# Experts of block 1: a ring of eleven weight slots until the fourth pair, and gathers and projections queued behind a pair's last input matmul

## The chip, the cores and the metric

The kernel runs on one core of a Trainium2 chip. The metric is the device time of one execution in microseconds (us). TensorE (PE) does the matmuls, VectorE (DVE), ScalarE (ACT) and GpSimd (POOL) the elementwise work, and SyncE (SP) issues the transfers of weights from HBM to SBUF, in one queue that is worked off in its order.

## The reference

Two blocks follow one another. Each mixes 256 tokens of width 1024 and then runs a layer of experts. The change touches the experts of block 1, 32 of them in four groups, with two chosen for each token in one group:

```python
for e in range(N_EXPERTS):
    a = jax.nn.silu(tok @ w_gate[e]) * (tok @ w_up[e])     # 1024 -> 512, twice
    out = out + combine[:, e:e + 1] * (a @ w_down[e])      # 512 -> 1024
```

`combine` holds the router's two weights of a token and zeros. Block 2's mixer needs projections of a second input, the context, which do not depend on block 1:

```python
h_ctx @ w_in        # one part of it, "xbc", is computed beside the experts of block 1
```

## The kernel before

**Pairs of experts.** `block1_moe` works through 16 pairs of experts. Each expert takes at most 32 tokens at first (a loop over a list, at L1685, does the others; it runs no iteration here). For a pair, PE multiplies the gathered tokens by eight *input pieces* of weights of 1 MB each (in0 to in3, for expert a and expert b; L1584). The *gated chain* follows: DVE L1471, three ACT operations, DVE L1473 and L1474, the transpose L1483 on PE, and the copy to `aT` on ACT. Then come four *output pieces* (out0, out1, each a and b; L1607), the multiplication into `y` on DVE, and the sum over tokens, `combine` (L1499 on PE, L1505 on DVE). `pd` and L1597 prepare the matrix for it.

**The weights' slots.** `Weights` holds the 1 MB pieces. `fetch` issues the next piece of a fixed list into the next slot of a fixed list: first the `first` slots, then the `ring` again and again. `n`, `w`, `za`, `zb`, `l`, `m`, `h0` and so on are names of regions in SBUF, and a piece's DMA waits on SP until the work that read that region before is done. Since SP has one queue, all that stands behind waits too. At pair 3 (`OVER`) the kernel fetches ahead what the loop over the list may disturb, runs the loop, and goes on with a ring of eight slots: `l` and `m` leave it, and `h1`, `g`, `g` join it.

**The gathers.** `Gather` picks the tokens of a range of experts with a one-hot matmul (L1352, `select` and `gather`, k = 0 to 7 for eight slices of the width). Experts 0 to 7 are gathered inside pair 0, 8 to 23 after pair 1's combine, and 24 to 31 after pair 2's.

**The context's projections.** `early()` takes the next step of `block2_ctx`. From pair 3 (`EARLY`) on it is called twice a pair: after the gated chain is written, and after the combine. A step issues two 0.5 MB loads `w_xbc` on SP (L365), splits them on ACT (L374) and DVE (L375), and multiplies them on PE: 32 matmuls of L403 and 16 of L407 a pair.

**Order on the engines.** A scheduler orders the instructions of each engine by its own estimates. `behind(pr, i)` tells it to put what is issued inside it after instruction `i`, where both are on one engine; it adds no wait of its own.

Of the kernel before, what the change touches and what calls it, by code (L numbers as in the profile page):

```python
# [28 lines left out]
EARLY = 3  # L29
# [504 lines left out]
def spread(pr, name, t):  # L534

    ap = pr.gains[name]
    pr.nc.sync.dma_start(t, bass.AP(tensor=ap.tensor, offset=ap.offset, ap=[[0, 128], [1, 1024]]))
    return t
# [819 lines left out]
class Gather:  # L1358
# [23 lines left out]
        gathered(self.pr, self.xhl, self.P, 32 * lo, 32 * hi - 32 * lo, self.gain, self.shift, k,  # L1382
                 self.tiles[key][:, o:o + 32 * hi - 32 * lo])

    def run(self, lo, hi):
        self.select(lo, hi)
        for k in range(8):
            self.gather(lo, hi, k)

    def __call__(self, k, e):  # L1390
# [45 lines left out]
def block1_weights(pr):  # L1436
    def piece(pi, s, j):
        for e in (2 * pi, 2 * pi + 1):
            yield (pi, s, j), pr.ins["wi" if s == "in" else "wd"][e, j]

    def order():


        for pi in range(16):
            js = [("in", k2) for k2 in range(4)] + [("out", h) for h in range(2)]
            for s, j in js if pi else js[:1] + js[4:] + js[1:4]:
                yield from piece(pi, s, j)
    ring = ["n"] * 2 + ["w"] * 3 + ["l", "m"]
    return order(), ["n"] * 2 + ["za"] * 3 + ["zb"] * 2 + ring[2:] + ["h0", "h1", ("hx", "hx"), ("zd", "y")], ring


def block2_weights(pr):
# [36 lines left out]
def behind(pr, i):  # L1489

    return pr.tc.issue_after(i.ins) if i is not None else nullcontext()
# [18 lines left out]
def block1_moe(pr, early):  # L1510
    nc, ins = pr.nc, pr.ins
    x = pr.x
    m1 = pr.mod1.rearrange("p (s k r) -> p s k r", s=6, r=2)
    gain, shift = (lambda k: pr.A2[:, k:k + 1]), (lambda k: m1[:, 3, k, 0:1])
    L = pr.L
    xhl = normed_split(pr, x, pr.r2)
    gl, el = L[:, :, 0:4], L[:, :, 4:36]
    b2 = lambda t, n: t[:, :, None].to_broadcast([128, 2, n])
    t2 = lambda n: pr.small(2, n)
    r3 = lambda t, n: t[:, 0:2 * n].rearrange("p (t e) -> p t e", t=2)  # L1520

    gm, gs, gw = t2("gm"), t2("gs"), t2("gw")
    nc.vector.tensor_reduce(gm, gl, AX.X, OP.max)
    ge = r3(pr.small(8, "ge8"), 4)
    nc.vector.tensor_sub(ge, gl, b2(gm, 4))
    nc.scalar.activation(ge, ge, AF.Exp)
    nc.vector.tensor_reduce(gs, ge, AX.X, OP.add)
    nc.vector.reciprocal(gw, gs)
    og = r3(pr.small(8, "og8"), 4)
    onehot_first(pr, og, gl, gm)  # L1530
    nc.vector.tensor_scalar(og, og, -1.0, -NEG, op0=OP.add, op1=OP.mult)

    em = pr.small(64, "em")
    e4 = em.rearrange("p (t g e) -> p t g e", t=2, g=4)
    nc.vector.tensor_add(e4, el.rearrange("p t (g e) -> p t g e", g=4),
                         og[:, :, :, None].to_broadcast([128, 2, 4, 8]))
    em = r3(em, 32)
    O, W, E = (pr.keep([128, 2, 32], n) for n in ("O", "W", "E"))
    m8 = pr.small(16, "m8").rearrange("p (t j) -> p t j", t=2)
    for t in range(2):  # L1540
        nc.vector.max(m8[:, t], em[:, t])
    two = pr.small(16, "two").rearrange("p (t j) -> p t j", t=2)
    nc.gpsimd.memset(two, -2.0 * NEG)
    nc.vector.tensor_copy(two[:, :, 0:2], m8[:, :, 0:2])
    for t in range(2):
        nc.vector.match_replace(E[:, t], two[:, t], em[:, t], 3.0 * NEG)
    nc.vector.tensor_tensor(O, E, em, op=OP.not_equal)
    pos = pr.keep([128, 2, 32], "pos")
    positions(pr, pos, O, 32)

    wb = t2("wb")
    nc.vector.tensor_sub(wb, m8[:, :, 1], m8[:, :, 0])
    nc.scalar.activation(wb, wb, AF.Exp)
    nc.vector.tensor_scalar(wb, wb, 1.0, None, op0=OP.add)
    nc.vector.reciprocal(wb, wb)
    nc.vector.tensor_mul(wb, wb, gw)
    nc.vector.tensor_sub(W, em, b2(m8[:, :, 0], 32))
    nc.scalar.activation(W, W, AF.Exp)
    nc.vector.tensor_mul(W, W, b2(wb, 32))
    nc.vector.tensor_mul(W, W, O)  # L1560
    pr.dbg("combine", W)
    xe = Gather(pr, pos, xhl, 32, gain, shift, [(("xa", "zc"), 0, 8), (("za", "za"), 8, 24), (("za",), 24, 32)])
    g2 = spread(pr, "g2", pr.new("g2", "g2"))
    moe = pr.moe[0]
    for pi in range(16):
        if pi == OVER:
            moe.fetch(7)
            overflow(pr, li, pos, W, xhl, gain, shift, x, g2)

            for tag in ("l", "m"):  # L1570
                moe.ring.remove(tag)
            moe.ring.extendleft(["h1", "g", "g"])
        es = (2 * pi, 2 * pi + 1)
        p = pr.ps("d")
        if pi == 0:
            xe.select(0, 8)
        for k2 in range(4):
            w = moe.take(pi, "in", k2)
            for k in (2 * k2, 2 * k2 + 1):
                if pi == 0:  # L1580
                    xe.gather(0, 8, k)
                for g in range(4):
                    e = es[g % 2]
                    nc.tensor.matmul(p[32 * g:32 * g + 32], xe(k, e), w[g % 2][2 * (g // 2) + k % 2],  # L1584
                                     start=k == 0, stop=k == 7, tile_position=(0, 32 * g))
        a = gated(pr, p, 64)
        if pi >= EARLY:
            early()
        aT = down_inputs(pr, a, 64)
        p = pr.ps("t")  # L1590
        for t in range(2):
            v = xe.P[t][:, 64 * pi:64 * pi + 64].rearrange("p (e j) -> p e j", e=2)
            d = pr.small(128, "pd")
            nc.gpsimd.tensor_mul(d.rearrange("p (e r j) -> p e r j", e=2, r=2),
                                 v[:, :, None, :].to_broadcast([128, 2, 2, 32]),
                                 W[:, t, 2 * pi:2 * pi + 2, None, None].to_broadcast([128, 2, 2, 32]))
            nc.tensor.transpose(p[:, 128 * t:128 * t + 128], d, pr.ident)  # L1597
        PWT = pr.small(256, "PWT")
        nc.scalar.activation(PWT, p[:, 0:256], AF.Copy)
        y = pr.new("y", "y")  # L1600
        for h in range(2):
            p = pr.ps("m")
            w = moe.take(pi, "out", h)
            for i in range(2):
                for g in range(4):
                    z = 64 * (2 * (g % 2) + i) + 32 * (g // 2)
                    nc.tensor.matmul(p[32 * g:32 * g + 32], aT[:, z:z + 32], w[g // 2][2 * (g % 2) + i],  # L1607
                                     start=i == 0, stop=i == 1, tile_position=(0, 32 * g))
            nc.vector.tensor_mul(y[:, 512 * h:512 * h + 512], p, g2[:, 512 * h:512 * h + 512])
        for h in range(2):  # L1610
            combine(pr, x, PWT, y, h, False, then=last if pi == 15 else None)
        if pi in (1, 2):
            xe.run(*((8, 24), (24, 32))[pi - 1])
        if pi == 0:
            li = overflow_list(pr, O)
        if pi >= EARLY:
            early()
        if pi == 4:
            fg = bcast(pr, "fin", pr.new("g2", "fg"))
        if pi == 14:  # L1620
            ss = pr.small(8, "s12").rearrange("p (n t h) -> p n t h", n=2, t=2)
            xf = []

            def last(t, z):

                if not xf:
                    xf.extend(pr.pair("P", "xf"))
                h = z.start // 512
                pr.squares(x[t][:, z], ss[:, 0, t, h:h + 1])
                nc.vector.tensor_mul(xf[t][:, z], x[t][:, z], fg[:, z])  # L1630
                pr.squares(xf[t][:, z], ss[:, 1, t, h:h + 1])


    m = pr.small(4, "m12")
    nc.vector.tensor_reduce(m.rearrange("p (n t) -> p n t", n=2), ss, AX.X, OP.add)
    nc.vector.tensor_scalar(m, m, 1.0 / 1024, None, op0=OP.mult)
    nc.vector.tensor_scalar(m[:, 0:2], m[:, 0:2], EPS, None, op0=OP.add)
    nc.vector.scalar_tensor_tensor(m[:, 2:4], m[:, 0:2], EPS, m[:, 2:4], op0=OP.mult, op1=OP.add)
    rr = pr.small(4, "r12")
    pr.rsqrt(rr, m)  # L1640
    pr.open.clear()
    pr.xh = pr.whole("w", "xn")
    nc.vector.tensor_scalar(pr.xh[0], xf[0], rr[:, 2:3], None, op0=OP.mult)
    nc.scalar.activation(pr.xh[1], xf[1], AF.Copy, scale=rr[:, 3:4])
    for t in range(2):
        nc.vector.tensor_scalar(x[t], xf[t], rr[:, t:t + 1], None, op0=OP.mult)
        pr.dbg(f"x1_{t}", x[t])
# [728 lines left out]
```

## Time and profile before

| | before |
|---|---|
| median of 3 runs | 1987.08 us (1985.21 to 1988.03) |
| profiled execution | 1986.82 us, span of the trace 1985.0 us |
| PE / DVE / ACT / POOL busy | 85% / 50% / 35% / 16% |
| mean granted clock of TensorE | 0.922 |
| moved by the DMA engines | 576.67 MB, mean 291 GB/s |

The span is what the trace covers, and all times below count from its start. Block 1's experts lie between 638 and 1168 us, and the loop over the list at 740 us divides them: all engines meet there. "Ahead of the loop" and "after the loop" mean this point. A granted clock of 1.00 is TensorE's full clock, 0.5 half of it.

### The profile page before, as it was taken

How to read it: one execution, taken by the hardware profiler on the slowest of the kernel's cores; microseconds unless marked ns; L12 is line 12 of the kernel's file. 1: busy time of each engine (PE TensorE's matmuls, PEld its weight loads, DVE VectorE, ACT ScalarE, POOL GpSimd, SP SyncE). 2: the span in 40 equal slices, each digit the busy share in tenths (PEclk: the TensorE clock that was granted, in tenths of full speed). 3: DMA queues.
4: the chain of work that ended last, by engine and by line, in shares of the span. 5: the costliest groups of instructions: out<-in, count | busy, mean ns of one | idle time of the engine just before them, and what ended most of it. 6: DMA issues, size and time to landing. Idle time of an engine off the chain costs nothing.

```text
span 1985.0 us, 30710 instructions
## 1 busy us (share of the span) xinstructions
PE 1695.2 (85%) x12402; PEld 1094.5 (55%) x12402; DVE 997.6 (50%) x1805; ACT 699.6 (35%) x1201; POOL 320.8 (16%) x353
## 2 busy tenths in 40 slices
PE   6999999999998966887878769988997878778766
PEld 3988888898997312343433239988995222111111
DVE  3678988886875224233333249689753221111112
ACT  4455554445544303122221136544644211111111
POOL 0123544200012000000000004256311000000000
PEclk7999999999998988898989889989997988889888
DMA  9554445453656689999999974445656999999996
GB/s 351 205 210 171 181 161 200 155 208 119 221 199 235 269 334 401 402 389 421 392 377 376 420 305 150 161 145 187 234 180 246 400 419 420 420 420 421 420 421 274
DMA packets 108159, 576.67 MB, mean 291 GB/s; under 512 B 12296, under 2 KB 13040, under 8 KB 62064
## 3 DMA queue, kind: packets, MB, share of 16 engines
q1 hardware_dynamic: 103536, 561.59, 72.2%
q10 hardware_dynamic: 4480, 13.11, 1.8%
q8 instruction: 98, 1.61, 0.3%
q14 instruction: 45, 0.37, 0.1%
HBM read 573.52 MB, written 1.13 MB: 289 GB/s over the span
## 4 chain that ended last, share of the span: by engine, by line
PE 58%; DMA 20%; DVE 13%; ACT 6%; issue 2%; POOL 1%; SPq 0%; ACTq 0%; DVEq 0%
PE psd L403 13%; DMA we<-wu 10%; PE psd L433 7%; PE psd L407 7%; PE psm L1607 6%; PE psd L1584 5%; PE psm L1499 3%; DMA we<-wd 3%; DMA we<-wi 3%; PE psd L2283 3%; PE psm L2304 2%; DMA we<-wg 2%; DVE R L2070 2%; DVE hl L375 2%; PE psd L462 2%
## 5 line engine op out<-in xcount | busy, mean ns | idle before, releaser
L403 PE MATMUL psd<-hT,hl 128*128 128x256 f32 x2304 | 322.5, 289 | 7.1 <-ACT hl L374 5.0
L403 PEld LDWEIGHTS psd<-hT,hl 128*128 128x128 f32 x2304 | 288.3, 191 | 48.2 <-issue 30.1
L375 DVE TENSOR_TENSOR hl<-w,hl 128x1024 fp32r<-128x1024 f32 (+1 forms) x203 | 256.3, 1264 | 86.8 <-ACT hl L374 86.1
L374 ACT ACTIVATE hl<-w 128x1024 fp32r<-128x1024 f32 (+1 forms) x203 | 211.2, 1041 | 250.8 <-PE psd L407 155.7
L2283 PE MATMUL psd<-we,xe 128*32 128x512 f32 x1024 | 169.3, 613 | 29.9 <-DMA we<-wu 23.9
L407 PE MATMUL psd<-hT,hl 128*128 128x256 f32 x1152 | 171.7, 290 | 5.8 <-DVE hl L375 5.8
L1584 PE MATMUL psd<-we,xe 128*32 128x512 f32 x1024 | 157.1, 624 | 20.7 <-DMA we<-wi 20.6
L407 PEld LDWEIGHTS psd<-hT,hl 128*128 128x128 f32 x1152 | 149.2, 192 | 16.2 <-issue 9.3
L611 ACT ACTIVATE zs<-z 64x512 f32<-64x512 f32 x32 | 20.2, 630 | 350.6 <-DVE z L1471 350.6
L433 PE MATMUL psd<-hl,hT 128*128 128x256 f32 x1056 | 137.7, 288 | 4.1 <-DVE hl L375 2.4
L433 PEld LDWEIGHTS psd<-hl,hT 128*128 128x128 f32 x1056 | 131.2, 193 | 8.5 <-DVE hl L375 2.6
L1483 PE MATMUL pst<-cst,zs 64*128 64x64 f32 x128 | 20.0, 300 | 133.5 <-DVE zs L1474 133.5
L1471 DVE TENSOR_SCALAR z<-psd 64x512 f32<-64x512 f32 x32 | 21.8, 682 | 221.5 <-PE psd L2283 143.6
L1499 PE MATMUL psm<-y,PWT 128*128 128x512 f32 x256 | 132.4, 624 | 0.9 <-DVE x L1505 0.9
L1505 DVE TENSOR_TENSOR acc<-acc,psm 128x512 f32<-128x512 f32 x60 | 41.3, 688 | 180.8 <-PE psm L1499 180.8
L1607 PE MATMUL psm<-we,aT 128*32 128x512 f32 x512 | 112.7, 755 | 7.6 <-ACT aT L1485 7.6
L2283 PEld LDWEIGHTS psd<-we,xe 128*32 128x32 f32 x1024 | 34.2, 110 | 146.6 <-issue 79.3
L1483 PEld LDWEIGHTS pst<-cst,zs 64*128 64x128 f32 x128 | 14.4, 190 | 161.5 <-DVE zs L1474 152.1
L2304 PE MATMUL psm<-we,aT 128*32 128x512 f32 x512 | 96.1, 843 | 7.6 <-ACT aT L1485 7.6
L1584 PEld LDWEIGHTS psd<-we,xe 128*32 128x32 f32 x1024 | 33.5, 113 | 104.2 <-issue 79.3
L1499 PEld LDWEIGHTS psm<-y,PWT 128*128 128x128 f32 x256 | 40.1, 188 | 82.3 <-issue 51.5
L2290 POOL TENSOR_SCALAR pd<-P,W 128x128 f32<-128x128 f32 x32 | 19.3, 614 | 400.0 <-PE pst L2293 396.8
(527 smaller groups left out, 2561.0 us busy)
## 6 DMA issues: line engine op xcount, KB each, us to landing
we<-wi SPq DMA_DIRECT2D x126, 1024.0 KB
we<-wd SPq DMA_DIRECT2D x120, 1024.0 KB
we<-wu SPq DMA_DIRECT2D x57, 1024.0 KB
we<-wg SPq DMA_DIRECT2D x56, 1024.0 KB
w<-w_in SPq DMA_DIRECT2D x80, 512.0 KB
w<-w_ada SPq DMA_DIRECT2D x48, 512.0 KB
w<-w_mod SPq DMA_DIRECT2D x48, 512.0 KB
w<-w_xbc SPq DMA_DIRECT2D x36, 512.0 KB
```

The lines of the kernel that those rows point to most:

```text
L374: nc.scalar.activation(t[:, 0:w], raw[:, :w], AF.Copy)
L375: nc.vector.tensor_sub(t[:, w:2 * w], raw[:, :w], t[:, 0:w])
L403: mm(out, w(0, k), H[k][:, i], start=start and a == 0 and k == 0 and i == 0, stop=False, skip_group_check=True)
L407: mm(out, w(1, k), H[k][:, 0], start=False, stop=stop and k == n - 1, skip_group_check=True)
L433: mm(out, act(a, 4 * kh + k, t), w(b, k), start=kh == 0 and i == 0 and n == 0 and k == 0, stop=kh == 1 and i == 2 and k == 3, skip_group_c ...
L462: nc.tensor.matmul(p[32 * g:32 * g + 32, :256], sil[:, 4 * h + g, :], w[:, g], start=h == 0, stop=h == 1, tile_position=(0, 32 * g))
L1499: nc.tensor.matmul(p, PWT[0:rows, 128 * t:128 * t + 128], y[0:rows, 512 * h:512 * h + 512], start=True, stop=True)
L1505: nc.vector.tensor_add(a, a, p)
L1584: nc.tensor.matmul(p[32 * g:32 * g + 32], xe(k, e), w[g % 2][2 * (g // 2) + k % 2], start=k == 0, stop=k == 7, tile_position=(0, 32 * g))
L1607: nc.tensor.matmul(p[32 * g:32 * g + 32], aT[:, z:z + 32], w[g // 2][2 * (g % 2) + i], start=i == 0, stop=i == 1, tile_position=(0, 32 * g))
L2283: nc.tensor.matmul(p[32 * g:32 * g + 32], xe(k, e), w[g // 2][2 * (g % 2) + k % 2], start=k == 0, stop=k == 7, tile_position=(0, 32 * g))
L2304: done = nc.tensor.matmul(p[32 * g:32 * g + 32], aT[:, z:z + 32], w[g // 2][2 * (g % 2) + i], start=i == 0, stop=i == 1, tile_position=(0, ...
```

## The change

Until pair 3 the ring has eleven slots instead of seven: the two of `zb` and `h0`, `h1` are added, and taken out again before the fetch ahead of the loop, so that the ring behind the loop is the one of before. The pieces of pair 0 come in another order: the second half of its output, out1b, goes from the fourth place to the last, and the list of first slots is reordered to fit. The gathers of experts 8 to 31 are spread over pairs 0, 1 and 2, and stand *behind* a pair's last input matmul, and so does the first `early()` call of every pair from 3 on.

```diff
--- before.py
+++ after.py
@@ -1382,9 +1382,10 @@
         gathered(self.pr, self.xhl, self.P, 32 * lo, 32 * hi - 32 * lo, self.gain, self.shift, k,
                  self.tiles[key][:, o:o + 32 * hi - 32 * lo])
 
-    def run(self, lo, hi):
-        self.select(lo, hi)
-        for k in range(8):
+    def run(self, lo, hi, k0=0, k1=8):
+        if k0 == 0:
+            self.select(lo, hi)
+        for k in range(k0, k1):
             self.gather(lo, hi, k)
 
     def __call__(self, k, e):
@@ -1441,12 +1442,14 @@
     def order():
 
 
-        for pi in range(16):
-            js = [("in", k2) for k2 in range(4)] + [("out", h) for h in range(2)]
-            for s, j in js if pi else js[:1] + js[4:] + js[1:4]:
-                yield from piece(pi, s, j)
-    ring = ["n"] * 2 + ["w"] * 3 + ["l", "m"]
-    return order(), ["n"] * 2 + ["za"] * 3 + ["zb"] * 2 + ring[2:] + ["h0", "h1", ("hx", "hx"), ("zd", "y")], ring
+        js = [("in", k2) for k2 in range(4)] + [("out", h) for h in range(2)]
+        one = [p for j in js for p in piece(0, *j)]
+        yield from one[0:2] + one[8:11] + one[2:8] + one[11:12]
+        for pi in range(1, 16):
+            for j in js:
+                yield from piece(pi, *j)
+    ring = ["n"] * 2 + ["zb"] * 2 + ["w"] * 3 + ["l", "m", "h0", "h1"]
+    return order(), ["n"] * 2 + ["za"] * 3 + ring[2:8] + [("zd", "y")] + ring[8:] + [("hx", "hx")], ring
 
 
 def block2_weights(pr):
@@ -1564,6 +1567,8 @@
     moe = pr.moe[0]
     for pi in range(16):
         if pi == OVER:
+            for tag in ("zb", "zb", "h0", "h1"):
+                moe.ring.remove(tag)
             moe.fetch(7)
             overflow(pr, li, pos, W, xhl, gain, shift, x, g2)
 
@@ -1581,11 +1586,15 @@
                     xe.gather(0, 8, k)
                 for g in range(4):
                     e = es[g % 2]
-                    nc.tensor.matmul(p[32 * g:32 * g + 32], xe(k, e), w[g % 2][2 * (g // 2) + k % 2],
-                                     start=k == 0, stop=k == 7, tile_position=(0, 32 * g))
+                    mm = nc.tensor.matmul(p[32 * g:32 * g + 32], xe(k, e), w[g % 2][2 * (g // 2) + k % 2],
+                                          start=k == 0, stop=k == 7, tile_position=(0, 32 * g))
         a = gated(pr, p, 64)
-        if pi >= EARLY:
-            early()
+
+        with behind(pr, mm):
+            if pi >= EARLY:
+                early()
+            else:
+                xe.run(*((8, 24, 0, 4), (8, 24, 4, 8), (24, 32, 0, 8))[pi])
         aT = down_inputs(pr, a, 64)
         p = pr.ps("t")
         for t in range(2):
@@ -1609,8 +1618,6 @@
             nc.vector.tensor_mul(y[:, 512 * h:512 * h + 512], p, g2[:, 512 * h:512 * h + 512])
         for h in range(2):
             combine(pr, x, PWT, y, h, False, then=last if pi == 15 else None)
-        if pi in (1, 2):
-            xe.run(*((8, 24), (24, 32))[pi - 1])
         if pi == 0:
             li = overflow_list(pr, O)
         if pi >= EARLY:
```

On SP ahead of the loop, names that begin with `we` are pieces, and `li` is the list that the loop reads. Before, from pair 1's output pieces to the read of the list (7759, 7761, 7773 and 7775 are pair 1's output, 7851 to 7865 and 7887 pair 2's input):

```order
L1401 DMA we_7759<-wd 128x2048
L1401 DMA we_7761<-wd 128x2048
L1401 DMA we_7773<-wd 128x2048
L1406 DMA we_7699<-wi 128x1024
L1401 DMA we_7775<-wd 128x2048
L1401 DMA we_7851<-wi 128x2048
L1401 DMA we_7853<-wi 128x2048
L1401 DMA we_7863<-wi 128x2048
L1401 DMA we_7887<-wi 128x2048
L1401 DMA we_7865<-wi 128x2048
L1684 TENSOR_LOAD li_7678
```

The last three input pieces of pair 2 (7875, 7877, 7889) stand behind the read of the list, and behind them the rest of pair 2's output:

```order
L1684 TENSOR_LOAD li_7678
L1684 ISA x2
L1401 DMA we_7925<-wd 128x2048
L1401 DMA we_7875<-wi 128x2048
L1401 DMA we_7877<-wi 128x2048
L1401 DMA we_7889<-wi 128x2048
L1401 DMA we_7927<-wd 128x2048
```

After, the same stretch on SP (7992 is the last output piece of pair 2, 7657 the second half of pair 0's out1b, 8015 and 8017 are pair 3's first input):

```order
L1402 DMA we_7992<-wd 128x2048
L1407 DMA we_7657<-wd 128x1024
L1402 DMA we_7877<-wi 128x2048
L1402 DMA we_7887<-wi 128x2048
L1402 DMA we_8015<-wi 128x2048
L1402 DMA we_8017<-wi 128x2048
L1691 TENSOR_LOAD li_7707
L1691 ISA x2
L1402 DMA we_7889<-wi 128x2048
L1402 DMA we_7976<-wd 128x2048
L1402 DMA we_7978<-wd 128x2048
L1402 DMA we_7990<-wd 128x2048
```

Only one input piece of pair 2 (7889) is left behind the list. Half of pair 0's out1b is now queued behind pair 2's last output piece.

On PE after the loop, in pair 6's combine and pair 7's input, 8931 to 8969 are input pieces and `hl` the context's weights. Before:

```order
L1499 MATMUL psm_8898<-y_8866,PWT_8864 128x512
L1584 MATMUL psd_8930<-we_8931,xe_7800 32x512
L403 MATMUL psd_8993<-hT_8323,hl_8922 128x256 x8
L403 MATMUL psd_8993<-hT_8344,hl_8922 128x256 x8
L1499 MATMUL psm_8901<-y_8866,PWT_8864 128x512
L407 MATMUL psd_8993<-hT_8323,hl_8922 128x256
L1499 MATMUL psm_8904<-y_8866,PWT_8864 128x512
L407 MATMUL psd_8993<-hT_8323,hl_8922 128x256 x3
L407 MATMUL psd_8993<-hT_8344,hl_8922 128x256 x4
L403 MATMUL psd_8993<-hT_8323,hl_8927 128x256 x7
L1584 MATMUL psd_8930<-we_8933,xe_7800 32x512
```

The 48 context matmuls stand between the combine and the input matmuls, and the list goes on with input pieces up to the transpose L1483. After, from behind the last input matmul on:

```order
L1774 MATMUL pst_8987<-cst,xb_8907 128x128 x4
L403 MATMUL psd_8993<-hT_8323,hl_8922 128x256 x8
L403 MATMUL psd_8993<-hT_8344,hl_8922 128x256 x8
L407 MATMUL psd_8993<-hT_8323,hl_8922 128x256 x4
L407 MATMUL psd_8993<-hT_8344,hl_8922 128x256 x4
L403 MATMUL psd_8993<-hT_8323,hl_8927 128x256 x8
L403 MATMUL psd_8993<-hT_8344,hl_8927 128x256 x8
L407 MATMUL psd_8993<-hT_8323,hl_8927 128x256 x4
L407 MATMUL psd_8993<-hT_8344,hl_8927 128x256 x4
L1486 MATMUL pst_9042<-cst,zs_8980 128x64 x4
L1606 MATMUL pst_9049<-cst,pd_9050 128x128
L1606 MATMUL pst_9049<-cst,pd_9053 128x128
L1616 MATMUL psm_9059<-we_9060,aT_9047 32x512 x2
```

They now stand together, after the last input matmul and ahead of the transpose L1483 of the gated chain, and the transposes of `pd` no longer break up the output matmuls.

## Rows read from the trace of the kernel before

**Rows 1.** The page: engines, and the chain that ended last.

```profile
PE 1695.2 (85%) x12402; PEld 1094.5 (55%) x12402; DVE 997.6 (50%) x1805; ACT 699.6 (35%) x1201; POOL 320.8 (16%) x353
...
PE 58%; DMA 20%; DVE 13%; ACT 6%; issue 2%; POOL 1%; SPq 0%; ACTq 0%; DVEq 0%
```

**Rows 2.** Windows after the loop; last columns: granted clock, DMA share, GB/s.

```profile
770.00:1102.00 332.00, 269.94 (x1567) 113.80 (x1561) 115.50 (x187) 74.32 (x133) 16.64 (x26) 0.89 0.97 393
865.00:932.00 67.00, 55.56 (x334) 23.54 (x333) 23.05 (x36) 15.64 (x27) 4.51 (x8) 0.91 1.01 420
1035.00:1070.00 35.00, 29.63 (x170) 12.92 (x170) 9.84 (x19) 6.35 (x14) 1.98 (x3) 0.89 0.90 366
1102.00:1134.00 32.00, 25.37 (x127) 7.01 (x125) 6.20 (x9) 3.43 (x7) 1.20 (x3) 0.88 1.01 421
```

**Rows 3.** Waits of PE from 745 to 1165: total, times, longest.

```profile
PE pst L1483 <- DVE zs L1474: 63.1, 13, 5.5
PE psd L1584 <- DMA we<-wi: 11.6, 6, 6.3
```

**Rows 4.** Groups of PE in five pairs, 865 to 1036, shapes apart.

```profile
L1584 PE MATMUL psd<-we,xe 128*32 128x512 f32 x320 | 47.6, 597 | 0.0
L1607 PE MATMUL psm<-we,aT 128*32 128x512 f32 x160 | 33.6, 767 | 2.4 <-ACT aT L1485 2.4
L403 PE MATMUL psd<-hT,hl 128*128 128x256 f32 x160 | 24.2, 293 | 0.0
...
L407 PE MATMUL psd<-hT,hl 128*128 128x256 f32 x80 | 16.5, 333 | 0.0
...
L1483 PE MATMUL pst<-cst,zs 64*128 64x64 f32 x18 | 3.0, 309 | 21.0 <-DVE zs L1474 21.0
```

**Rows 5.** Timeline of PE, pair 6 to pair 7.

```profile
864.47 0.69 PE L1483 MATMUL pst<-cst,zs 64*128 64x64 f32 x4 [5.02 <-DVE zs L1474]
...
876.63 2.18 PE L403 MATMUL psd<-hT,hl 128*128 128x256 f32 x16
...
887.48 5.35 PE L1584 MATMUL psd<-we,xe 128*32 128x512 f32 x46
897.84 0.34 PE L1483 MATMUL pst<-cst,zs 64*128 64x64 f32 x2 [5.01 <-DVE zs L1474]
```

**Rows 6.** Timeline of PE: pairs 5 and 12.

```profile
831.79 0.68 PE L1483 MATMUL pst<-cst,zs 64*128 64x64 f32 x4 [5.45 <-DVE zs L1474]
...
1071.39 0.69 PE L1483 MATMUL pst<-cst,zs 64*128 64x64 f32 x4 [5.05 <-DVE zs L1474]
```

**Rows 7.** Windows without transfers, ahead of the loop.

```profile
641.20:644.50 3.30, 3.30 (x18) 1.04 (x18) 0.00 (x0) 0.86 (x2) 0.00 (x0) 0.87 0.06 10
667.50:678.00 10.50, 10.50 (x58) 3.70 (x59) 2.07 (x3) 2.48 (x4) 0.40 (x1) 1.00 0.00 0
697.00:702.00 5.00, 5.00 (x28) 1.16 (x21) 0.69 (x1) 0.00 (x0) 0.40 (x1) 0.69 0.00 0
```

**Rows 8.** Timeline of PE, pairs 1 and 2, to the loop.

```profile
689.72 0.50 PE L1352 MATMUL psg<-P,hi 128*128 128x256 f32 x2
...
696.43 3.40 PE L1607 MATMUL psm<-we,aT 128*32 128x512 f32 x10 [0.47 <-ACT aT L1485]
...
713.47 1.92 PE L1584 MATMUL psd<-we,xe 128*32 128x512 f32 x14 [0.57 <-DMA we<-wi]
...
720.63 3.56 PE L1607 MATMUL psm<-we,aT 128*32 128x512 f32 x10 [0.47 <-ACT aT L1485]
...
740.35 5.24 PE L1584 MATMUL psd<-we,xe 128*32 128x512 f32 x28 [8.14 <-DMA we<-wi]
```

**Rows 9.** Timeline of SP's queue: DMAs issued, count last.

```profile
701.24 0.33 SPq L1401 DMA_DIRECT2D we<-wd  x1
...
725.45 14.93 SPq L1401 DMA_DIRECT2D we<-wi  x5
```

## The prediction

> **What bounds the kernel now.** I read the page first: PE is busy 85% of the span and holds 58% of the chain that ended last, the DMA engines 20% [rows 1]. That average hides the stage of the change, so I read its stretches. After the loop, from 770 to 1102 us, the DMA engines moved 393 GB/s. In the pairs from 865 to 932 they moved 420, with the same mixture of loads, and in the pairs without context loads 421; in a slow stretch 366 [rows 2]. So the transfers are the near bound of this stage, and they are not always fed.
>
> What starves them is PE. Its waits there are not for weights, 11.6 us, but for the gated chain: 63.1 us in 13 pairs, 4.85 each [rows 3]. One pair shows the pattern: the context's matmuls stand among and ahead of the input matmuls (876.63), the input is done late, PE then idles 5.0 us until the chain arrives (897.84), and only then come the output matmuls, whose slots the next transfers need [rows 5]. From pair 5 to pair 12 the transposes L1483 are 239.6 us apart over seven pairs, 34.2 us a pair [rows 6]. A pair's transfers are twelve pieces of 1.05 MB and two of 0.52, 13.6 MB, which at 421 GB/s take 32.4 us (2.5 us a piece). So PE's sequence is 1.8 us a pair longer than the transfers.
>
> Ahead of the loop it is plainer. There are stretches of 3.3, 10.5 and 5.0 us with next to no transfers [rows 7], and the last of them ends with SP issuing at 701.24 [rows 9], after pair 1's output matmuls began at 696.43 and freed a slot. Pair 2's input, held up by that, ends at 715.4, its output starts at 720.63, and at 725.45 that frees slots for the last pieces ahead of the loop [rows 8, 9]. PE waits 8.14 us for them and goes on at 740.35 [rows 8].
>
> **The change, ahead of the loop.** The bytes are the same; only what can be issued early changes. By the order, one input piece of pair 2 is left behind the slots of pair 1's output, where there were three and an output piece ahead of them. Two effects oppose each other.
>
> First the loss. Half of pair 0's out1b now stands in SP's queue behind pair 2's last output piece, whose slot comes free only with pair 2's first input matmuls. Ahead of it fourteen pieces go out without a gap from 644.5, the end of the first empty stretch [rows 7]; at 2.5 us each it lands at 644.5 + 14.5 × 2.5 = 681. By the durations of before, my estimate is that PE has all else that it may do behind it at about 675, so it waits some 6.5 us. That stall replaces most of what PE gains by starting pair 0 earlier, so pair 1's output starts at about 698.0, 1.5 us later than 696.43.
>
> Then the gain. Four pieces went out from 701.24 on, and the last input piece among them set the end of the input at 715.4. With one piece in place of four that end is 3 × 2.5 = 7.5 us nearer to pair 1's output; less the 1.5 us it lies at 709.4. Behind it now stand the gathers of experts 24 to 31. A slice is four matmuls of 256 columns; by the row at 689.72 and the three like it, two slices take 1.4 us with a short wait, so eight take about 5.3 us [rows 8]. They cover the gated chain, which took the 5.2 us from 715.4 to 720.63, and with some 2 us of pair 1's combine left in front, pair 2's output starts near 716.7 instead of 720.63. What follows, slots, last pieces and loop, moves with it: **4 us**. Bounds: a stall for out1b longer by 5 us would make it −1; at the other end, half of the 18.8 us of empty queue [rows 7] would be 9. I take 4, because the end hangs on pair 2's output and not on the queue alone.
>
> **The change, after the loop.** The same pieces go into the same eight slots. What moves is PE's order. Per pair the context's matmuls cost (24.2 + 16.5) / 5 = 8.1 us, the input 47.6 / 5 = 9.5, the output 33.6 / 5 = 6.7 [rows 4]. Put behind the last input matmul, the 8.1 us fill the 5.0 us in which PE idled, and leave the front of the next pair. With L the landing of a pair's last input piece: the input ends at L + 1, the context at L + 9, the transpose, the copy and the first output matmuls follow at L + 11, and the first output slot is free at about L + 13. The transfer that needs this slot is the eighth piece later, due at L + 8 × 2.5 = L + 20. So there is a cover of about 7 us. PE then still has the combine and 7 us of input matmuls to do before the next L, at L + 32.4, and is done by about L + 28. The transfers set the period: 32.4 us where there was 34.2.
>
> The worth is read from the transfers, since PE cannot end earlier than they do: 332 us × (1 − 393/421) = 22.1 us from 770 to 1102 [rows 2]. I take **20 us**, because the queue has to fill again behind the loop, and because the splits of the next context weights stand ahead of `aT` on ACT and ahead of `y` on DVE, at a microsecond or so inside the cover. Bounds: 10 us, if the period falls only to the 33 us of the pairs that ran well before; 24, if the stretches next to this one gain too. The `pd` transposes ahead of the output matmuls and the two adjacent `w_xbc` loads lie in the same cover; without it each would cost below 1 us a pair. Block 2 keeps its order and moves earlier.
>
> The sum, against the profiled execution: 1986.8 − 4 − 20 = **1962.8, so 1963 us**. That execution is 0.3 us from the median, which I neglect.
>
> **A rule against this.** In the stretch that the sum extends, the transfers ran at 420 GB/s for 67 us [rows 2]. The Trainium skill, "DMA: Bandwidth & Descriptors", section "Where 436 GB/s comes from", says that from HBM to SBUF the HBM side binds, at about 358 GB/s for a core. By it a stretch at 393 could not shrink, and 1982.8 would be left. The trace contradicts that with 420; it agrees with "HBM Reference", section "Specifications (TRN2)", by which a core that streams alone measures about 425.
>
> **The rivals.**
>
> *Little after the loop.* Something else, such as a slot freed late by another reader, or transfers that don't keep 420, leaves the period near where it was. For it: even at a DMA share of 0.97 the rate was only 393 [rows 2]. Against it: the 865 to 932 stretch. With none of the second term it is 1982.8, with half of it 1972.8. Chance 0.20, of which 0.01 is for a rate that itself cannot rise, as that rule has it.
>
> *No change.* The order on PE is moved but the period stays 34.2, because TensorE falls to half clock more often in the new order. PE is busy for 29.6 of the 35 us of the slow stretch, at a granted clock of 0.89 [rows 2], so some 5 us more of busy time a pair would be enough. A clock below 1.00 says that it falls already. The term ahead of the loop is then eaten by a stall for out1b some 4 us longer than mine. About 1987. Chance 0.07.
>
> *Slower.* The context's matmuls delay the output past the cover. If they run at half clock, 16 us, and the gated chain's 5 us follow them instead of running beside them, the output starts near L + 23 and frees its slot at L + 25, 5 us late. The period becomes 37.4, and over the eight pairs with context loads that is 8 × 3.2 = 26 us lost; less 4 it ends near 2008. The point from which it decides is a slot late by more than 1.8 us, that is, an output that starts 9 us later than I have it. Against it: the chain waits for nothing of the context. Chance 0.07.
>
> *Better.* Both upper bounds come in: 1986.8 − 9 − 24 = 1954. Chance 0.04.
>
> **How the numbers follow.** My case, both terms at about their size, 1955 to 1972, has 0.62. The range reaches from the upper bounds, 1953, to 1980, which takes in most of the case of little after the loop, and leaves out its worst end, no change and slower: about 0.2. A measurement of this kernel tells about 0.2%, 4 us, from no change. Faster is 0.62 + 0.20 + 0.04 = 0.86, same 0.07, slower 0.07.
>
> **What would show it.** In the profile after, right: the loop ends near 736; the period from pair 5 to pair 12 is 32 to 33 us, and the windows there read 410 to 421 GB/s; PE's wait for DVE L1474 shrinks to little, and a wait of PE for input pieces takes its place, several us a pair. Also a wait of PE of 5 to 8 us near 675 to 681 for an output piece. Wrong: PE still waits little for pieces after the loop, or the windows there stay below 400; or an output piece's slot is what SP waits for with idle queues.

## The result, and the profile after

The changed kernel took 1955.33 us (median of 4 runs, 1953.84 to 1960.14) beside 1986.14 for the kernel before, a ratio of 0.9858 with a 95% interval of 0.9838 to 0.9879. In a second set of runs, beside the last experiments, it was 0.9879 (0.9863 to 0.9896). So it is 1.2% to 1.4% faster, 24 to 28 us. The profiled execution took 1960.14 us, 26.7 below the one of before, where 24 were forecast. The other three runs of the first set were 4 to 6 us below this one; those of the second set took 1958.02 to 1960.86 us.

Not all of the 26.7 us belong to the change. All times count from a trace's own start, and the first gather of the experts, ahead of which nothing was changed, came 3.0 us earlier in the trace after (second line) than in the one before (first line):

```profile
634.97 0.77 PE L1352 MATMUL psg<-P,hi 128*128 128x256 f32 x2 [1.62 <-DVE P L1340]
```

```profile
631.95 0.76 PE L1352 MATMUL psg<-P,hi 128*128 128x256 f32 x2 [1.62 <-DVE P L1340]
```

In the traces of this study it lies between 630.75 and 636.75, and kernels that are alike up to there show 631.95 as well as 636.46. So where two traces are compared below, it is from this first gather on.

The chain that ended last, to be read beside [rows 1], is taken from the second profile of the changed kernel; in the first it can be followed back only to 397 us, so that its shares are of another stretch.

```profile
PE 51%; DMA 29%; DVE 12%; ACT 5%; issue 2%; POOL 1%; SPq 0%; ACTq 0%; DVEq 0%
```

PE's part of the chain fell from 58% to 51%, and that of the DMA engines rose from 20% to 29%. Where it changed is seen in the stretches after the loop, which answer to [rows 2] (the last columns are the granted clock, the DMA share and GB/s):

```profile
832.00:1035.00 203.00, 171.81 (x1038) 74.36 (x1030) 69.53 (x112) 49.42 (x86) 11.89 (x18) 0.95 1.01 421
1035.00:1070.00 35.00, 30.59 (x196) 14.10 (x196) 11.08 (x22) 8.44 (x17) 1.99 (x3) 1.00 1.01 421
```

From 832 us on the transfers run at 421 GB/s, pair after pair, where they had run at 366 to 420. PE's waits from 740 to 1140, which answer to [rows 3], changed places:

```profile
PE psd L1589 <- DMA we<-wi: 43.7, 29, 9.9
PE pst L1486 <- DVE zs L1477: 17.1, 4, 4.4
```

PE now waits 43.7 us for input pieces, and for the gated chain only in four pairs, none of them one with context matmuls behind its input. One pair shows how, beside [rows 5]:

```profile
907.76 1.46 PE L1589 MATMUL psd<-we,xe 128*32 128x512 f32 x10
...
909.57 2.16 PE L403 MATMUL psd<-hT,hl 128*128 128x256 f32 x16
...
914.45 1.12 PE L407 MATMUL psd<-hT,hl 128*128 128x256 f32 x8
915.50 0.46 PE L1486 MATMUL pst<-cst,zs 64*128 64x64 f32 x4
...
917.50 3.64 PE L1616 MATMUL psm<-we,aT 128*32 128x512 f32 x32 [1.18 <-ACT aT L1488]
...
934.75 1.92 PE L1589 MATMUL psd<-we,xe 128*32 128x512 f32 x14 [1.43 <-DMA we<-wi]
```

The context's 48 matmuls start 0.35 us after the last input matmul (907.76 + 1.46) and end where the transpose L1486 begins, with no idle time ahead of it. The output starts at 917.50, 8.3 us after the input's end. Then PE does the combine and the next input, and waits 1.43 us for a piece (934.75). From pair 5 to pair 12 the transposes are now 225.5 us apart over seven pairs, 32.2 a pair, where it was 34.2 [rows 6]:

```profile
818.28 0.46 PE L1486 MATMUL pst<-cst,zs 64*128 64x64 f32 x4
...
1043.76 0.46 PE L1486 MATMUL pst<-cst,zs 64*128 64x64 f32 x4
```

With the hole the clock changed too. The stretch of a pair's output behind PE's wait of 5 us, before (first line), was granted 0.63; the one without such a wait, after (second line), 1.00:

```profile
864.40:873.00 8.60, 8.06 (x38) 2.38 (x42) 0.70 (x2) 1.26 (x3) 1.16 (x3) 0.63 1.02 427
```

```profile
915.90:922.00 6.10, 4.92 (x37) 1.42 (x36) 4.72 (x8) 4.17 (x8) 0.02 (x1) 1.00 1.00 414
```

Ahead of the loop, pair 0 to the loop on PE, beside [rows 8]:

```profile
666.06 2.30 PE L1589 MATMUL psd<-we,xe 128*32 128x512 f32 x13
...
680.52 3.47 PE L1616 MATMUL psm<-we,aT 128*32 128x512 f32 x10 [2.79 <-DMA we<-wd]
...
697.31 0.69 PE L1486 MATMUL pst<-cst,zs 64*128 64x64 f32 x4 [7.17 <-DVE zs L1477]
698.47 3.62 PE L1616 MATMUL psm<-we,aT 128*32 128x512 f32 x10 [0.47 <-ACT aT L1488]
...
709.25 1.92 PE L1589 MATMUL psd<-we,xe 128*32 128x512 f32 x14
...
717.91 1.92 PE L1616 MATMUL psm<-we,aT 128*32 128x512 f32 x16
...
734.06 9.16 PE L1589 MATMUL psd<-we,xe 128*32 128x512 f32 x64 [8.25 <-DMA we<-wi]
```

PE goes on behind the loop at 734.06 instead of 740.35. Counted from the first gather that is 102.1 us instead of 105.4. So of the 26.7 us the start gave 3.0, the stretch ahead of the loop 3.3, and the one from there to the end of the last output matmul of the experts (first line before, second line after) 20.3:

```profile
1165.60 1.92 PE L1607 MATMUL psm<-we,aT 128*32 128x512 f32 x16
```

```profile
1139.06 1.92 PE L1616 MATMUL psm<-we,aT 128*32 128x512 f32 x16
```

### The profile page after: what moved, and what is told of

It reads as the page before. It is cut to its first block, busy times and chain, and to the rows that moved or that the text cites. A ratio compares the mean times of both kernels' runs of the same rounds, so it can differ in the third digit from the quotient of the medians.

```text
span 1958.3 us, 30719 instructions
## 1 busy us (share of the span) xinstructions
PE 1672.6 (85%) x12402; PEld 1087.2 (56%) x12402; DVE 993.3 (51%) x1805; ACT 698.9 (36%) x1201; POOL 322.1 (16%) x353
## 4 chain that ended last, share of the span: by engine, by line
PE 37%; DMA 28%; DVE 8%; ACT 4%; issue 1%; POOL 1%; SPq 0%; ACTq 0%; DVEq 0%
DMA we<-wi 13%; PE psd L403 9%; DMA we<-wu 8%; DMA we<-wd 5%; PE psd L407 5%; PE psd L433 4%; PE psm L1616 3%; PE psd L2290 3%; PE psd L1589 3%; DMA we<-wg 3%; PE psm L2311 2%; DVE R L2077 2%; PE psm L1502 2%; DVE hl L375 1%; PE psg L1352 1%
## 5 line engine op out<-in xcount | busy, mean ns | idle before, releaser
L403 PE MATMUL psd<-hT,hl 128*128 128x256 f32 x2304 | 314.3, 288 | 5.8 <-ACT hl L374 4.6
L1589 PE MATMUL psd<-we,xe 128*32 128x512 f32 x1024 | 172.9, 657 | 52.0 <-DMA we<-wi 51.9
L2290 PE MATMUL psd<-we,xe 128*32 128x512 f32 x1024 | 169.3, 613 | 32.2 <-DMA we<-wu 25.4
L1474 DVE TENSOR_SCALAR z<-psd 64x512 f32<-64x512 f32 x32 | 21.9, 683 | 328.2 <-PE psd L1589 165.5
L407 PE MATMUL psd<-hT,hl 128*128 128x256 f32 x1152 | 164.3, 285 | 5.8 <-DVE hl L375 5.8
L2311 PE MATMUL psm<-we,aT 128*32 128x512 f32 x512 | 94.5, 830 | 7.6 <-ACT aT L1488 7.6
L1616 PE MATMUL psm<-we,aT 128*32 128x512 f32 x512 | 83.6, 658 | 14.0 <-ACT aT L1488 11.2
L1486 PE MATMUL pst<-cst,zs 64*128 64x64 f32 x128 | 18.2, 279 | 88.8 <-DVE zs L1477 87.0
L913 POOL TENSOR_TENSOR za<-za,qz 128x512 f32<-128x512 f32 x28 | 63.6, 2285 | 115.7 <-ACT za L909 115.7
```

Source lines behind the costliest of these rows:

```text
L403: mm(out, w(0, k), H[k][:, i], start=start and a == 0 and k == 0 and i == 0, stop=False, skip_group_check=True)
L407: mm(out, w(1, k), H[k][:, 0], start=False, stop=stop and k == n - 1, skip_group_check=True)
L913: nc.gpsimd.tensor_mul(Q, Q, q)
L1589: mm = nc.tensor.matmul(p[32 * g:32 * g + 32], xe(k, e), w[g % 2][2 * (g // 2) + k % 2], start=k == 0, stop=k == 7, tile_position=(0, 32 * g))
L2290: nc.tensor.matmul(p[32 * g:32 * g + 32], xe(k, e), w[g // 2][2 * (g % 2) + k % 2], start=k == 0, stop=k == 7, tile_position=(0, 32 * g))
L2311: done = nc.tensor.matmul(p[32 * g:32 * g + 32], aT[:, z:z + 32], w[g // 2][2 * (g % 2) + i], start=i == 0, stop=i == 1, tile_position=(0, ...
```

## The experiments

In this table the columns of pair 1's output and of the loop count from the first gather, and the last column is the time from the end of the loop to the end of the last output matmul. The two traces of the changed kernel differ by 0.4 us at most.

| trace | first gather at | pair 1's output starts | loop left | loop to last output |
|---|---|---|---|---|
| before | 634.97 | 61.5 | 105.4 | 427.2 |
| changed kernel | 631.95 | 66.5 | 102.1 | 406.9 |
| changed kernel, second trace | 632.72 | 66.3 | 102.0 | 406.5 |
| ring alone | 633.41 | 67.6 | 102.9 | 430.1 |
| context calls alone | 632.85 | 61.4 | 105.9 | 408.8 |
| gathers alone | 632.38 | 58.9 | 102.5 | 425.8 |
| changed, list early | 630.75 | 54.4 | 86.9 | 407.8 |
| changed, pieces in the old order | 632.33 | 59.6 | 90.9 | 407.1 |
| changed, list early and old order | 633.51 | 58.3 | 89.8 | 406.8 |
| changed without the ring | 636.75 | 56.4 | 101.2 | 407.1 |
| changed without the ring, list early | 632.00 | 51.7 | 98.9 | 409.9 |
| before, list early | 632.14 | 52.7 | 98.7 | 426.8 |

**The ring alone.** The kernel before with the edits to `block1_weights` and to the ring at `OVER`. The diff is cut; the new order of pair 0's pieces and of the first slots is in it as well.

```diff
-    ring = ["n"] * 2 + ["w"] * 3 + ["l", "m"]
+    ring = ["n"] * 2 + ["zb"] * 2 + ["w"] * 3 + ["l", "m", "h0", "h1"]
...
+            for tag in ("zb", "zb", "h0", "h1"):
+                moe.ring.remove(tag)
```

> Only the ring of eleven slots and the new order of pair 0's pieces; gathers and context projections where they were. My theory: it acts ahead of the loop alone. The pair's period after the loop stays at 34.2 us, the loop ends 0 to 6 us earlier than 740.35, and the time is 0 to 6 us below before. Rival, that the deeper ring gives most of the gain: 20 us or more below before, with 420 GB/s after the loop.

Measured: 1983.57 us beside 1984.09, ratio 0.9999 (0.9986 to 1.0011). No difference, as expected, and after the loop the transfers stay below 400 GB/s (second row). But the idle queue ahead of the loop had not gone away (first row):

```profile
690.00:707.00 17.00, 10.13 (x52) 4.61 (x55) 7.30 (x25) 4.88 (x9) 0.40 (x1) 0.70 0.00 0
832.00:1035.00 203.00, 169.18 (x1002) 73.81 (x1002) 70.83 (x112) 47.77 (x84) 11.88 (x18) 0.91 0.98 399
```

The eleven slots are filled early, and then the queue stands still for 17 us, because the slots free themselves as late as before. On PE pair 1's output starts 6.1 us later than before, counted from the first gather, though the loop is left 2.5 us earlier. In this trace the stretch after the loop is 2.9 us longer than before, so that nothing is left; why was not taken apart.

```profile
701.03 3.62 PE L1611 MATMUL psm<-we,aT 128*32 128x512 f32 x10 [0.47 <-ACT aT L1487]
...
736.35 4.48 PE L1588 MATMUL psd<-we,xe 128*32 128x512 f32 x20 [8.28 <-DMA we<-wi]
```

**The context calls alone.** The kernel before with the edit below; `mm` is kept from the input matmul, as in the change.

```diff
-        if pi >= EARLY:
-            early()
+        with behind(pr, mm):
+            if pi >= EARLY:
+                early()
```

> Only the first context call of a pair goes behind the last input matmul; ring, order of pieces and gathers as before. My theory: the loop ends at 740 as before, the period from pair 5 to pair 12 falls to 32.3 us, the windows after the loop read 420 GB/s, and the time is 18 to 22 us below before. Rival, that the new order only pays with the deeper ring: less than 8 us.

Measured: 1964.06 us, ratio 0.9898 (0.9880 to 0.9916), 20 us faster, with the old ring. The transfers read 420 GB/s over the whole stretch for which [rows 2] has 393, and PE waits for input pieces:

```profile
770.00:1102.00 332.00, 273.71 (x1656) 114.72 (x1654) 115.82 (x191) 75.05 (x134) 17.77 (x28) 0.95 1.01 420
```

```profile
PE psd L1584 <- DMA we<-wi: 46.1, 28, 11.1
```

The trace puts 18.4 us of it after the loop. So nearly all of the gain after the loop is this one edit's, without the deeper ring.

**The gathers alone.** The kernel before with `xe.run(...)` spread over pairs 0 to 2, behind `mm`.

> Only the gathers of experts 8 to 31 are spread and go behind the last input matmul of pairs 0, 1 and 2; ring and context calls as before. My theory: PE's idle time in the gated chain ahead of the loop is filled, but the transfers are limited by the ring of seven; the loop ends 0 to 4 us earlier, 0 to 4 us below before. Rival, that the gathers and not the ring bring the 6.3 us that the loop ended earlier: 6 us below before, with the ring alone at 0.

Measured: 1977.73 us, ratio 0.9974 (0.9960 to 0.9987), 5.2 us faster. The interval, 2.6 to 7.9 us, takes in both the rival's 6 us and most of my 0 to 4, so the time does not decide between them. The trace says more: counted from the first gather, pair 1's output starts 2.6 us earlier than before and the loop is left 2.9 us earlier, which is nearly the 3.3 of the whole change. In that the rival was right.

```profile
691.24 3.32 PE L1611 MATMUL psm<-we,aT 128*32 128x512 f32 x10 [0.47 <-ACT aT L1486]
...
734.85 8.86 PE L1585 MATMUL psd<-we,xe 128*32 128x512 f32 x64 [9.64 <-DMA we<-wi]
```

**The list of overflowing experts moved.** Comparing the two traces, I had found pair 1's chain waiting on DVE. These are DVE's rows in the changed kernel:

```profile
684.02 0.69 DVE L1618 TENSOR_TENSOR y<-psm,g 128x512 f32<-128x512 f32 x1 [9.29 <-PE psm L1616]
...
689.20 0.19 DVE L1666 COPY cnt<-psm 128x32 f32<-128x32 f32 x1 [1.72 <-PE psm L1664]
...
693.15 0.68 DVE L1474 TENSOR_SCALAR z<-psd 64x512 f32<-64x512 f32 x1
```

DVE waits 9.29 us for the late half of pair 0's output and multiplies it into `y` (684.02), adds to `x`, works out the list from 689.20 on (19 operations, where the expectation below says 24), and between its last operations takes pair 1's first operation of the gated chain, L1474, at 693.15. The experiment issues the list at the start of pair 0, ahead of all that:

```diff
         if pi == 0:
             xe.select(0, 8)
+            li = overflow_list(pr, O)
...
-        if pi == 0:
-            li = overflow_list(pr, O)
```

> The changed kernel with the list of overflowing experts worked out at the start of pair 0 and not behind its combine. In the changed kernel 24 small operations of it stand on DVE ahead of pair 1's first operation of the gated chain, which starts at 693.15 though PE's input ended at 690.1. My theory: pair 1's output starts about 2 us earlier, and the loop ends 2 us earlier: 2 us below the changed kernel. Rival, that the slots or the transfers set that end: no change within 1 us.

Measured: 1941.92 us, ratio 0.9805 (0.9783 to 0.9826), 11 to 15 us below the changed kernel by its two ratios, where I had expected 2. I had taken the matmuls that end at 690.1 for pair 1's. They are pair 2's; pair 1's input ends at 668.4 (the row at 666.06 above), so its chain had stood on DVE for 25 us. That is far more than the 5 us of the list itself. With the list away DVE's order changes: L1474 comes at 667.10, as soon as PE has done the input, and no longer behind the late half of pair 0,

```profile
667.10 0.68 DVE L1474 TENSOR_SCALAR z<-psd 64x512 f32<-64x512 f32 x1 [3.17 <-PE psd L1590]
```

and on PE pair 1's transpose comes at 673.93, ahead of the late piece of pair 0 (679.20), instead of at 697.31:

```profile
673.93 0.46 PE L1486 MATMUL pst<-cst,zs 64*128 64x64 f32 x4
...
679.20 1.90 PE L1617 MATMUL psm<-we,aT 128*32 128x512 f32 x10 [0.49 <-DMA we<-wd]
...
685.13 1.87 PE L1617 MATMUL psm<-we,aT 128*32 128x512 f32 x12
...
717.61 9.76 PE L1590 MATMUL psd<-we,xe 128*32 128x512 f32 x64 [8.23 <-DMA we<-wi]
```

Pair 1's output then runs at 685, 12 us earlier counted from the first gather, and the loop is left 15 us earlier. What moved is the order on DVE that the scheduler gives; why it gives this one was not looked into.

**The pieces of pair 0 in the order of before, and both together.** The edit to the changed kernel; both together add the early list:

```diff
-        yield from one[0:2] + one[8:11] + one[2:8] + one[11:12]
+        yield from one[0:2] + one[8:12] + one[2:8]
```

> The changed kernel with all of pair 0's output pieces ahead of its input pieces in1 to in3, as before the change; the list stays behind pair 0's combine. In the changed kernel the late half of pair 0's out1b lands at 680, so pair 0's combine and the list end near 694, and pair 1's gated chain waits on DVE behind them from 668 to 693. My theory: with the piece early, combine and list end earlier and the chain with them, but the last input piece of pair 1 takes its late place in the queue; pair 1's output starts 0 to 9 us earlier, time 0 to 8 us below the changed kernel. Rival, that only the list's own 5 us on DVE matter: no change within 1 us.

Measured: 1949.84 us, ratio 0.9838 (0.9812 to 0.9863). Against 0.9858 and 0.9879 of the changed kernel that is 4 to 8 us, as expected, though the lower end is inside the intervals; the trace has 11 us at the loop. Pair 1's output starts 7 us earlier. So the late piece costs something by itself.

> The changed kernel with the list at the start of pair 0 and all of pair 0's output pieces ahead of in1 to in3. Alone they brought 13 and 4 us. Theory: both shorten the same stretch, from pair 0's output to pair 1's, so the sum is not reached; the late piece is then pair 1's in3b, which sets pair 1's chain again: as the early list alone, or a few us worse, 35 to 43 us below before. Rival, that they add: 46 us below before.

Measured: 1951.63 us, ratio 0.9834 (0.9815 to 0.9853), 33 us below before where 35 to 43 were expected. The two do not add; together they are some 6 us worse than the early list alone, 3 at the loop. With this order it is an input piece of pair 1 that comes late (by the list in3b), and its chain starts on DVE at 681.81, after a wait for PE, where the early list alone has 667.10:

```profile
681.81 0.68 DVE L1474 TENSOR_SCALAR z<-psd 64x512 f32<-64x512 f32 x1 [5.28 <-PE psd L1590]
```

**Is the ring worth anything?** In this part the ring is the eleven slots together with the new order of pieces. Three kernels answer. The changed kernel without its ring, and the same with the early list as well:

> The changed kernel without its ring part: ring of seven and the order of pieces of before, gathers and context calls as changed, the list behind pair 0's combine. Theory: while the list stands there the ring is worth nothing, so 25 to 28 us below before, within 3 us of the changed kernel. Rival, that the ring pays in the changed kernel too: 15 us or less below before.

> The changed kernel with the list at the start of pair 0, but the ring of seven slots and the order of pieces of before. Theory: the deeper ring is worth something, and in the changed kernel the list's place hid it. Then without the ring little of the 13 us that the early list brought is left: 0 to 4 us below the changed kernel, with idle queues of 15 us or more ahead of the loop. Rival, that the list's place alone brought it: 10 to 13 us below the changed kernel.

Measured: without the ring 0.9884 (0.9865 to 0.9903), 23 us below before, beside 0.9879 on the same chip for the changed kernel (of which 26 to 31 us had been expected in this second set, and 24 came). With the early list but without the ring 0.9873 (0.9852 to 0.9894), beside 0.9805 with both. So the ring is worth nothing while the list stands behind pair 0's combine, and some 13 us where it doesn't. Some 8 of these are there with the old order of pieces too (0.9834 beside 0.9873). Pair 1's output and the loop without the ring, list late:

```profile
693.11 3.62 PE L1612 MATMUL psm<-we,aT 128*32 128x512 f32 x10 [0.47 <-ACT aT L1486]
...
737.90 7.32 PE L1585 MATMUL psd<-we,xe 128*32 128x512 f32 x44 [9.68 <-DMA we<-wi]
```

and with the list early:

```profile
683.72 1.90 PE L1613 MATMUL psm<-we,aT 128*32 128x512 f32 x10 [0.47 <-ACT aT L1486]
...
730.91 9.16 PE L1586 MATMUL psd<-we,xe 128*32 128x512 f32 x64 [10.15 <-DMA we<-wi]
```

Counted from the first gather, pair 1's output starts 10 us earlier without the ring than in the changed kernel, yet the loop is left only 1 us earlier. The ring with its order delays pair 1's output and shortens what follows by nearly as much.

The early list in the kernel before:

> The kernel before with the list at the start of pair 0 and nothing else. Theory: the early list pays only where pieces are in SBUF for pair 1 to go on, so with the ring of seven 0 to 4 us below before. Rival, that it pays by itself: 10 us or more below before.

Measured: 1973.05 us, ratio 0.9949 (0.9935 to 0.9963), 10 us faster. Here the rival was right: the list pays by itself, some 9 us at the start of pair 1's output and 7 at the loop, counted from the first gather:

```profile
684.88 3.62 PE L1608 MATMUL psm<-we,aT 128*32 128x512 f32 x26
...
730.88 9.00 PE L1585 MATMUL psd<-we,xe 128*32 128x512 f32 x64 [8.09 <-DMA we<-wi]
```

Beside the moved gathers and the old ring it shrinks to some 2 us (0.9884 to 0.9873), which the intervals do not tell from nothing. The gathers probably have part of the same gain; how the two share it was not taken apart.

**The cover after the loop.** In the changed kernel, behind the context's matmuls of pairs 5 to 11, n more that nobody uses:

```diff
                 early()
+                if 5 <= pi <= 11:
+                    q = pr.ps("t")
+                    for _ in range(n):
+                        nc.tensor.matmul(q[:, 0:128], pr.ident, pr.ident, start=True, stop=True)
```

> The changed kernel with 30 more 128x128 matmuls, whose result is not used, behind the context's matmuls in pairs 5 to 11: some 5 us of PE work a pair. Theory: transfers set the period, PE has 32.4 less 27.6 = 4.8 us a pair to spare, and output slots come free about 8 us before they are due; so 0 to 5 us above the changed kernel over the seven pairs. Rival, that PE's sequence still sets the period: 7 x 5 = 35 us above it.

> The same with 60 such matmuls, some 10 us a pair, more than PE has to spare. Theory: the period rises by about 5 us in seven pairs, 30 to 40 us above the changed kernel, and the slots of output pieces are late. Rival, that only the slot's cover of 8 us counts and not the work: 5 to 15 us above it.

Measured: with 30 of them 1960.71 us, ratio 0.9880 (0.9857 to 0.9903), 0 to 4 us above the changed kernel by its two ratios; its window shows a PE that is hardly ever idle and transfers that hardly notice:

```profile
820.00:1040.00 220.00, 215.47 (x1522) 127.62 (x1523) 76.41 (x122) 54.32 (x92) 14.65 (x23) 1.00 1.01 416
```

The output starts 13.9 us after the input's end, and the period is 32.6 us all the same (from 824.65 to 1020.41 in six pairs). With 60 it is 2047.82 us, 1.0319 (1.0298 to 1.0341), 87 to 92 us above, far beyond both expectations:

```profile
820.00:1080.00 260.00, 234.05 (x1676) 149.78 (x1674) 68.37 (x107) 49.20 (x81) 11.91 (x18) 0.95 0.77 308
```

```profile
L1599 PE MATMUL pst<-cst 128*128 128x128 f32 x600 | 67.8, 275 | 0.0
L1589 PE MATMUL psd<-we,xe 128*32 128x512 f32 x319 | 51.9, 688 | 24.0 <-DMA we<-wi 24.0
```

Over five pairs the 60 matmuls took 67.8 us, 13.6 a pair, not 10; the trace counts two for each. The period is 45.3 us (from 837.59 to 1109.26 in six pairs), 13.1 over 32.2. PE's work comes to 234 / 260 of it, 41 us, so that it alone is some 9 us longer than the transfers. The rest, 4 to 5 us a pair, is waiting for pieces, 24.0 us in these five pairs. The output starts 23.9 us after the input's end; that its slots then come free too late for the pieces that are due would explain these waits, but no run separates it from PE's work.

## Why the prediction was right, and where not

The time lies in the range, and the forecast of 24 us met 23.6 in the profile, without the 3.0 of the start, and 24 to 28 in the runs.

**After the loop: right, by its steps.** 20 us forecast, 20.3 in the profile, and 20 from this edit alone. The period went to 32.2, forecast 32.4; the windows to 421, forecast 410 to 421; the wait moved from the gated chain to the pieces. The output came 8.3 us after the input's end, where I had 10: the context's matmuls took 283 to 285 ns each where they stand together, and 293 to 333 broken up [rows 4]. In five pairs of the changed kernel:

```profile
L1589 PE MATMUL psd<-we,xe 128*32 128x512 f32 x320 | 61.3, 682 | 17.6 <-DMA we<-wi 17.6
L403 PE MATMUL psd<-hT,hl 128*128 128x256 f32 x160 | 21.2, 285 | 0.0
...
L1616 PE MATMUL psm<-we,aT 128*32 128x512 f32 x160 | 18.2, 595 | 5.8 <-ACT aT L1488 5.8
L407 PE MATMUL psd<-hT,hl 128*128 128x256 f32 x80 | 11.2, 283 | 0.0
```

The context costs (21.2 + 11.2) / 5 = 6.5 us instead of 8.1, the output 3.6 instead of 6.7, at the full clock, and the input, which now waits for its pieces, 12.3 instead of 9.5 [rows 4]. The prediction counted on the hole alone, and its rival of no change on a clock that falls more often; the clock rose, from 0.91 to 0.95. The filled hole, 5.0 us a pair, and the shorter output, 3.1, are each more than the 1.8 us by which PE's sequence had been too long; no run tells them apart. The cover that I gave as about 7 us stands up: 6.8 us of extra work (half of the 13.6) cost next to nothing in the period, 13.6 did. So the slower rival's point of decision may well lie between the two, but with the 13.6 PE's work alone is longer than the transfers, and its late slots are not shown. The change does not come near either. The rival of little after the loop fell with the windows at 421. So did the rule of the Trainium skill ("DMA: Bandwidth & Descriptors", section "Where 436 GB/s comes from") that the prediction had set against itself.

**Ahead of the loop: the size met, partly by luck.** The term was 4 us and came out at 3.3. The step from pair 1's output to the end of pair 2's input held: it took 12.7 us instead of 19.0, 6.3 less, where 7.5 were forecast. But pair 1's output started 5 us later than before, counted from the first gather, and not 1.5. So pair 2's output started no earlier than before, 86.0 us behind the first gather instead of 85.7, where 3.9 us of gain were forecast. What the loop gained came from behind that: the output took 4.0 us instead of 7.7, a term that the prediction does not have. PE's idle time ahead of it was filled by the gathers, and the granted clock was 1.00 there (second line) instead of 0.62 (first line, before):

```profile
719.70:724.19 4.49, 4.02 (x15) 0.94 (x15) 0.00 (x0) 0.38 (x1) 0.00 (x0) 0.62 1.01 418
```

```profile
717.90:722.00 4.10, 4.10 (x35) 1.10 (x35) 0.69 (x1) 0.96 (x3) 0.00 (x0) 1.00 0.39 110
```

The wait for the late piece of pair 0 was 2.8 us, not 6.5, because PE had other matmuls to do until 677.7. The piece was not held by another's slot for long: SP issued it at 662.04, and it lay behind the earlier ones in the DMA engines' queue, which ran at 421 GB/s from 662 to 680.

The step that failed is "that stall replaces most of what PE gains by starting pair 0 earlier, so pair 1's output starts at about 698.0, 1.5 us later". The late piece did not act by PE's stall but by DVE's queue: there pair 0's late half, its combine and the list stood ahead of pair 1's chain, whose input had been done for 25 us. By the early list, with the same late piece, pair 1's output starts 12 us earlier; with the piece early and the list late, 7. The prediction does not name the list. It also did not see that the gathers alone bring pair 1's output 2.6 us forward and that with the ring it falls back. So the ring's 7.5 us, about right for the step that they stand for, were cancelled: alone the ring brought nothing, and what the change gained ahead of the loop is about what the gathers gain alone.

## What to carry to other kernels

Independent work belongs in the hole that a dependent chain leaves on an engine, not ahead of the matmuls that start the chain; here that one move brought some 20 of the 24 to 28 us, because it made PE's sequence of a pair shorter than its transfers. More buffers do nothing while something else in order, here VectorE's queue, holds the work that would empty them: moving a small list, which is wanted only at the loop, reordered that queue and turned the 0 of the ring and its order of pieces into some 13 us. The version with both, 1941.92 us, is the best of this study. Before times of two traces are compared, see that the part ahead of the change takes the same time in both. Where a stall is priced, follow the waiting operation's own queue too, and ask which pair an instruction belongs to before reading its end as the start of a chain.

## What the runs showed of the hardware

One core kept 421 GB/s for 203 us together (832 to 1035 in the changed kernel), with next to nothing but 1 MB and 0.5 MB loads in one queue, and no window of 30 us or more that was read stood above 422. The granted clock of TensorE followed its idle time: 0.91 where PE idled 5 us a pair, 0.95 with the hole filled, and 1.00 with 30 matmuls that serve nothing, at 215 of 220 us busy. Right behind PE's idle time in the gated chain, over stretches of 4 to 9 us, it read 0.62 and 0.63, and ten records of an output matmul took 3.56 us there, where sixteen took 1.92 at 1.00. The 30 matmuls cost next to nothing in time, since the transfers set the period.
